# A chunked RWKV-7 recurrence: from two 64-column products per head pair to one 128x128 product each, with the outputs summed in SBUF

## The chip, the core and the metric

The kernel runs on one core of a Trainium2 chip. The metric is the device time of one execution in microseconds (us). The times given are the median of three runs with the lowest and the highest; the profile is of one further execution, and its own time stands beside its span.

The engines are called as the profile calls them: PE is TensorE (matmuls; PEld is its loading of weights), DVE is VectorE, ACT is ScalarE, POOL is GpSimd, SP is SyncE, whose queue issues nearly all DMAs.

## The reference

One layer of a hybrid decoder on 512 prompt tokens and 8 single decode tokens (520 columns in all), D_MODEL 2048. A shared RMS norm and one wide projection `w_in` feed two branches, an RWKV-7 time-mixing branch with 16 heads of 64 and a Conformer convolution branch; both are projected, merged by sigmoid gates, projected again, and a per-layer embedding and a last RMS norm follow. The part that the change touches is the state recurrence of the RWKV branch over the prompt:

```python
def _wkv7_scan(S0, r, w, k, v, a, b):
    def step(S, inp):
        r_t, w_t, k_t, v_t, a_t, b_t = inp
        sa = jnp.einsum('bhij,bhj->bhi', S, a_t)
        S = S * w_t[:, :, None, :] + sa[..., None] * b_t[:, :, None, :] + v_t[..., None] * k_t[:, :, None, :]
        return S, jnp.einsum('bhij,bhj->bhi', S, r_t)
...
S, o = _wkv7_scan(wkv_prev, rf, hd(decay), kf, vf, -kk, kk * hd(a))
mu = jnp.mean(o, axis=-1, keepdims=True)
var = jnp.mean(jnp.square(o - mu), axis=-1, keepdims=True)
o = ((o - mu) * lax.rsqrt(var + GN_EPS)).reshape(Bn, T, D_A) * lnx_g + lnx_b
```

The kernel does not step through the tokens. It cuts the 512 prompt tokens into 8 chunks of 64 and does each chunk with matrix products; `S` is carried from chunk to chunk.

## The kernel before

**The stream of big products.** All projections run through `step` (lines 195 to 213). A step takes one 128x128 block of weights, split into a high and a low part (`wh`, `wl`), and two halves of 260 columns of the activations, split likewise (`xh`, `xl`, or `hi`, `lo`), and issues six matmuls at line 211. `gemm` (line 215) makes 16 or 8 steps into one output tile. The weights come as 512 KB loads (line 143); ScalarE writes the high part (line 154), VectorE the low part (through the helper at line 107, which the profile shows as line 67, as all calls through `Paced`).

**The order of the work.** TensorE's order is the order of the program text (line 73), and from line 349 on VectorE's too. Everything that is not the stream is written as generators: `wkv(p, box)` for each of the 8 head pairs, `conv` for the convolution, and the tail (`samples`, `lnorm`, `reload`). After each step of `gemm`, `tick()` (line 181) lets each generator go on: `yield n` waits n steps, `yield ROOM` waits until the kernel's own estimate of VectorE's time is less than 1 us ahead of that of TensorE. These estimates grow with the calls: `pe_work` adds 0.13 us for each matmul of more than 32 columns, `vec` a price for each VectorE operation.

**The recurrence, `wkv` (line 427).** A head pair lies on the 128 partitions: head 0 on 0 to 63, head 1 on 64 to 127 (`half(h)`). For each pair:

- Lines 511 to 522 make `ar[h]` and `bk`. Lines 531 to 545 multiply them in both heads and mask the results into `nba`, `nbr` (on the diagonal blocks of a zeroed 128x128, two buffers, line 411) and into the other half of `ar[h]`.
- Lines 547 to 597 invert the triangular 32x32 blocks: `nba` goes through DRAM (`nd`) into `ni`; `ti` starts from a constant, copied by ScalarE from `cst` (line 567); 31 steps on VectorE; back through DRAM (`td`) into `dtt`, transposed into `dt`. Lines 602 to 610 complete `ttb`, the 128x128 inverse of both heads.
- Lines 613 to 621 make `suv`, which holds for each head and chunk the state on one half of the partitions and the values `v` on the other. Lines 624 to 630 transpose `bk` into `bkt`.
- Lines 632 to 662 are the **chunk loop**, 8 chunks each. The opening block makes two products of 64 columns for both heads: one into `x`, one into `oc`. ScalarE copies the first to `xs` (line 641). Four steps later (`ly`; five for the last pair) the middle block multiplies by `ttb`, and ScalarE puts the result into `suv` (line 645). Four steps on, the closing block makes again two 64-column products per head, one that updates the state (`bkt`) and one that is added to `oc` in PSUM (`nbr`). VectorE writes the next state into `suv` (line 655), ScalarE scales it into `sf` (line 659), and after four more steps the next chunk opens.
- Lines 666 to 698 normalise `oc` by head and write the result to DRAM (`oa_d`).

PSUM: `aux` tiles of 512 f32 per partition, four buffers (line 79), shared by all small products; `oc` held one of them for the whole loop. SBUF: `gt` gives tiles from a shared ring of 14 buffers (line 352), `kq.tile(name=...)` a buffer of that name.

Of the kernel before, what the change touches and what calls it, by code (L numbers as in the profile page):

```python
# [9 lines left out]
F32 = mybir.dt.float32  # L10
F32R = mybir.dt.float32r
AF = mybir.ActivationFunctionType
ALU = mybir.AluOpType
# [4 lines left out]
P = 128  # L18
T = 520
NPR = 512  # L20
# [3 lines left out]
NCH = 8  # L24
# [10 lines left out]
C_ID, C_GM, C_RM, C_TT, N_CST = 0, 128, 320, 576, 832  # L35
# [35 lines left out]
def body(nc, tc, a):  # L71
    with ExitStack() as es:
# [20 lines left out]
        dma = nc.sync.dma_start  # L93
        act = nc.scalar.activation
# [8 lines left out]
        vec = Paced(nc.vector, lambda name, n: work(0.0069 * n if name == "reciprocal" else (0.2 if name == "scalar_tensor_tensor" else 0.14) + 0.00107 * n))  # L103
        gps = Paced(nc.gpsimd, lambda name, n: work(0.0014 * n if n > 64 else 0.05))
        pe = Paced(nc.tensor, pe_work)

        def tt(eng, out, x, y, op):
            eng.tensor_tensor(out, x, y, op=op)
# [119 lines left out]
        def half(h):  # L228
            return slice(64 * h, 64 * h + 64)
# [22 lines left out]
        o = pa.tile([P, 512], F32, name="aux", tag="aux")  # L252
# [24 lines left out]
        cst = cp.tile([P, N_CST], F32, name="cst")  # L277
# [5 lines left out]
        ttinit = cst[:, C_TT:C_TT + 256]  # L283

        def constants():
            dma(out=sums, in_=a["cst"][:, N_CST:].rearrange("p (a b) -> p a b", a=3))
            dma(out=prm, in_=a["prm"])
            dma(out=muss, in_=a["ssT"])
            dma(out=cst, in_=a["cst"][:, :N_CST])
# [6 lines left out]
        def aux(name="aux"):  # L296
            return pa.tile([P, 512], F32, name=name, tag="aux")
# [40 lines left out]
        raw = kq.tile([P, NCH, P], F32, name="bkt").rearrange("p c x -> p (c x)")[:, :T]  # L338
# [16 lines left out]
        def gt(name):  # L355
            return gp.tile([P, T], F32, name=name, tag="g")
# [54 lines left out]
        nbrs = [kq.tile([P, NCH, P], F32, name=f"nbr{i}") for i in range(2)]  # L411
        for x in (ttb, *nbrs):
            gps.memset(x, 0.0)
# [13 lines left out]
        def wkv(p, box):  # L427
# [101 lines left out]
            nbr = nbrs[p % 2]  # L529
            f2 = lambda x: x.rearrange("p c a t -> p c (a t)")  # L530
            for c0 in (0, 4):
                os = [aux().rearrange("p (c x) -> p c x", x=P) for _ in range(2)]
                for c in range(4):
                    for h in range(2):
                        pe.matmul(os[h][:, c, :], lhsT=bk[half(h), c0 + c].rearrange("p a t -> p (a t)"),
                                         rhs=ar[h][half(h), c0 + c].rearrange("p a t -> p (a t)"), start=True, stop=True)
                yield 1
                for h in range(2):
                    s, u, o = half(h), half(1 - h), os[h]
                    mk = lambda s, i, n: gmask[s, i:i + n].unsqueeze(1).to_broadcast([64, 4, n])  # L540
                    tt(vec, nba[s, c0:c0 + 4], o[s, :, h * 64:h * 64 + 64], mk(s, 0, 64), ALU.mult)
                    i = 64 * (1 - h)
                    tt(vec, nbr[s, c0:c0 + 4, h * 64:h * 64 + 64], o[s, :, i:i + 64], mk(s, 64, 64), ALU.mult)
                    tt(vec, f2(ar[h][u, c0:c0 + 4]), o[u], mk(u, 64 * h, P), ALU.mult)
                    yield ROOM

# [11 lines left out]
            bh = bk.rearrange("p c a t -> p c (a t)")  # L558
# [3 lines left out]
            for g in range(4):  # L562
                dma(out=ni[g * 32:(g + 1) * 32], in_=nd.rearrange("h c e s t -> (h c e) s t"))
            yield 14
            vec.memset(ni.rearrange("p s t -> p (s t)")[:, 0::33], 1.0)
            ti = kq.tile([P, 8, 32], F32, name="ti")
            act(ti.rearrange("p i t -> p (i t)"), ttinit, AF.Copy)
# [10 lines left out]
            dtt = kq.tile([P, NCH, 32], F32, name="dtt")  # L578
# [4 lines left out]
            dt = kq.tile([P, NCH, 32], F32, name="dt")  # L583
# [40 lines left out]
            bkt = kq.tile([P, NCH, P], F32, name="bkt")  # L624
            for c0 in (0, 4):
                o = aux().rearrange("p (c x) -> p c x", x=P)
                for c in range(4):
                    pe.transpose(o[:, c, :], bh[:, c0 + c, :], ident)
                act(bkt[:, c0:c0 + 4, :], o, AF.Copy)
            yield 7  # L630

            oc = aux("oc").rearrange("p (c x) -> p c x", x=64)
            sf = kq.tile([P, 64], F32, name="sf")
            for c in range(NCH):
                x = aux().rearrange("p (c x) -> p c x", x=64)
                for h in range(2):
                    pe.matmul(x[half(h), 0, :], lhsT=ar[h][:, c, h, :], rhs=suv[:, h, c, :], start=True, stop=True)
                for h in range(2):
                    pe.matmul(oc[half(h), c, :], lhsT=ar[h][:, c, 1 - h, :], rhs=suv[:, h, c, :], start=True, stop=False)
                xs = kq.tile([P, 64], F32, name="xs", bufs=2)  # L640
                act(xs, x[:, 0, :], AF.Copy)
                yield ly
                pe.matmul(x[:, 2, :], lhsT=ttb[:, c, :], rhs=xs, start=True, stop=True)
                for h in range(2):
                    act(suv[half(h), h, c, :], x[half(h), 2, :], AF.Copy)
                yield ly
                for h in range(2):
                    pe.matmul(x[half(h), 3, :], lhsT=bkt[:, c, h * 64:h * 64 + 64], rhs=suv[:, h, c, :], start=True, stop=True)
                for h in range(2):
                    pe.matmul(oc[half(h), c, :], lhsT=nbr[:, c, h * 64:h * 64 + 64], rhs=suv[:, h, c, :], start=False, stop=True)  # L650

                for h in range(2) if c + 1 < NCH else ():
                    s = half(h)
                    if c:
                        vec.scalar_tensor_tensor(suv[s, h, c + 1, :], x[s, 3, :], epl[s, c:c + 1], sf[s], op0=ALU.mult, op1=ALU.add)
                    else:
                        vec.tensor_scalar(suv[s, h, 1, :], x[s, 3, :], epl[s, 0:1], None, op0=ALU.mult)
                for h in range(2) if c + 1 < NCH else ():
                    act(sf[half(h)], suv[half(h), h, c + 1, :], AF.Copy, scale=epl[half(h), c + 1:c + 2])  # L659
                if c + 1 == NCH:  # L660
                    vec.scalar_tensor_tensor(sf, x[:, 3, :], epl[:, c:c + 1], sf, op0=ALU.mult, op1=ALU.add)
                yield ly
            flag["done"] = p
# [3 lines left out]
            o1 = gt("o1")[:, :NPR].rearrange("p (c x) -> p c x", x=64)  # L667
# [5 lines left out]
            tt(vec, o1, oc, bc(m[:, 0]), ALU.subtract)  # L673
            sq = gt("sq")[:, :NPR].rearrange("p (c x) -> p c x", x=64)
            act(sq, o1, AF.Square)
# [7 lines left out]
            for h in range(2):  # L683
                for e in range(2):
                    tt(vec, on[half(e), :, h * 64:h * 64 + 64], o1[half(h), e::2, :],
                       m[half(h), 1, e::2].unsqueeze(2).to_broadcast([64, 4, 64]), ALU.mult)
                yield ROOM
# [474 lines left out]
```

## Time and profile before

| | |
|---|---|
| Median of three runs | 1788.19 us (1786.9 to 1790.8) |
| The profiled execution: its time, its span | 1786.46 us, 1784.6 us |
| Mean granted clock of TensorE | 0.995 |
| TensorE busy | 1765.0 us, 15576 matmul passes |
| VectorE, ScalarE, GpSimd busy | 1227.9, 805.4, 200.5 us |
| Chunk loops run | from 202.9 us (first pair) to about 1121 us (last pair) |

In the views of groups a row gives line, engine, operation, tiles (out<-in), shape and count; then busy us and the mean ns of one; then the idle time of the engine before them and what ended it. The mean length of a matmul holds its fill and its way through the array, and neighbours overlap; what a matmul costs the stream is read from the starts. In the timeline a row gives start and length in us, engine, line, operation, tiles, shape and count.

### The profile page before, as it was taken

How to read it: one execution, taken by the hardware profiler on the slowest of the kernel's cores; microseconds unless marked ns; L12 is line 12 of the kernel's file. 1: busy time of each engine (PE TensorE's matmuls, PEld its weight loads, DVE VectorE, ACT ScalarE, POOL GpSimd, SP SyncE). 2: the span in 40 equal slices, each digit the busy share in tenths (PEclk: the TensorE clock that was granted, in tenths of full speed). 3: DMA queues.
4: the chain of work that ended last, by engine and by line, in shares of the span. 5: the costliest groups of instructions: out<-in, count | busy, mean ns of one | idle time of the engine just before them, and what ended most of it. 6: DMA issues, size and time to landing. Idle time of an engine off the chain costs nothing.

```text
span 1784.6 us, 37783 instructions
## 1 busy us (share of the span) xinstructions
PE 1765.0 (99%) x15576; PEld 1728.7 (97%) x15576; DVE 1227.9 (69%) x2307; ACT 805.4 (45%) x1524; POOL 200.5 (11%) x237
## 2 busy tenths in 40 slices
PE   9999999999999999999999999999999999999996
PEld 9999999999999999999999999999999999999996
DVE  7568898899898797887987977465444333335457
ACT  6735447356364463463463433454333222243344
POOL 1100100001001001010010333001122000011111
PEclk9999999999999999999999999999999999999998
DMA  7253232432332434324324444477556332253233
GB/s 236 79 135 94 83 116 81 123 97 86 111 105 76 125 99 97 111 81 113 100 85 110 136 143 137 144 229 238 183 188 191 119 112 92 94 201 95 86 105 109
DMA packets 121037, 220.49 MB, mean 124 GB/s; under 512 B 47888, under 2 KB 56208, under 8 KB 120864
## 3 DMA queue, kind: packets, MB, share of 16 engines
q1 hardware_dynamic: 119264, 216.47, 39.4%
q8 instruction: 122, 2.00, 0.5%
q10 hardware_dynamic: 1600, 1.60, 0.3%
q14 instruction: 51, 0.42, 0.1%
HBM read 188.69 MB, written 29.34 MB: 122 GB/s over the span
## 4 chain that ended last, share of the span: by engine, by line
PE 96%; DVE 2%; DMA 1%; issue 0%; ACT 0%; POOL 0%; POOLq 0%; DVEq 0%; ACTq 0%
PE mm L211 88%; PE aux L67 6%; PE aux L211 1%; PE oc L67 1%; DVE c L67 1%; DVE wl L67 0%; DMA c_d<-c 0%; DVE h L67 0%; DMA w<-in_win 0%; POOL h L67 0%; DMA x<-in_xT 0%; DVE rf L67 0%; DVE bv L67 0%; POOLq L1158 0%; PE aux L1056 0%
## 5 line engine op out<-in xcount | busy, mean ns | idle before, releaser
L154 ACT ACTIVATE wh<-w 128x512 fp32r<-128x512 f32 (+1 forms) x541 | 339.2, 628 | 559.8 <-PE mm L211 493.4
L211 PE MATMUL mm<-xh,wh 128*128 128x260 f32 x2784 | 584.2, 291 | 0.1
L211 PE MATMUL mm<-xh,wl 128*128 128x260 f32 x2784 | 562.0, 283 | 1.1 <-DVE wl L67 0.9
L211 PE MATMUL mm<-xl,wh 128*128 128x260 f32 x2784 | 561.5, 283 | 0.0
L67 DVE TENSOR_TENSOR wl<-w,wh 128x512 fp32r<-128x512 f32 (+1 forms) x541 | 374.5, 694 | 172.3 <-ACT wh L154 170.1
L211 PEld LDWEIGHTS mm<-xh,wh 128*128 128x128 f32 x2784 | 428.5, 189 | 11.5 <-ACT wh L154 0.6
L211 PEld LDWEIGHTS mm<-xh,wl 128*128 128x128 f32 x2784 | 428.9, 189 | 1.5 <-DVE wl L67 1.5
L211 PEld LDWEIGHTS mm<-xl,wh 128*128 128x128 f32 x2784 | 429.5, 189 | 0.1
L211 PE MATMUL mm<-hi,wl 128*128 128x260 f32 x1600 | 332.8, 283 | 0.0
L211 PE MATMUL mm<-hi,wh 128*128 128x260 f32 x1600 | 332.5, 283 | 0.0
L211 PE MATMUL mm<-lo,wh 128*128 128x260 f32 x1600 | 331.8, 282 | 0.0
L211 PEld LDWEIGHTS mm<-hi,wh 128*128 128x128 f32 x1600 | 251.5, 189 | 0.0
L211 PEld LDWEIGHTS mm<-lo,wh 128*128 128x128 f32 x1600 | 251.1, 188 | 0.0
L211 PEld LDWEIGHTS mm<-hi,wl 128*128 128x128 f32 x1600 | 250.1, 188 | 0.0
L67 DVE SCALAR_TENSOR_TENSOR c<-u,prm,c 128x482 f32<-128x482 f32 (+14 forms) x240 | 186.9, 779 | 3.6
L67 DVE TENSOR_TENSOR p<-mm,rs 128x520 f32<-128x520 f32 x78 | 54.0, 693 | 53.7 <-PE mm L211 52.6
L67 DVE TENSOR_TENSOR tm<-ti,ni 128x16 f32<-128x16 f32 (+30 forms) x248 | 77.2, 311 | 5.7
L67 DVE TENSOR_REDUCE ti<-tm 128x8 f32<-128x16 f32 (+30 forms) x248 | 73.6, 297 | 8.5
L67 POOL TENSOR_TENSOR sq<-hi,lo 128x520 f32<-128x520 f32 (+1 forms) x20 | 26.8, 1344 | 353.7 <-DVE one L67 184.0
L67 DVE TENSOR_TENSOR s<-mm,s 128x520 f32<-128x520 f32 x32 | 22.4, 700 | 61.2 <-PE mm L211 61.2
L659 ACT ACTIVATE sf<-suv,epl 64x64 f32<-64x64 f32 x112 | 38.6, 345 | 56.7 <-DVE suv L67 55.2
L67 DVE SCALAR_TENSOR_TENSOR suv<-aux,epl,sf 64x64 f32<-64x64 f32 x96 | 27.1, 283 | 53.9 <-PE aux L67 51.8
(235 smaller groups left out, 1542.3 us busy)
## 6 DMA issues: line engine op xcount, KB each, us to landing
w<-in_win SPq DMA_DIRECT2D x170, 512.0 KB, 3.7
w<-in_wout SPq DMA_DIRECT2D x32, 512.0 KB, 3.7
w<-in_wpg SPq DMA_DIRECT2D x24, 512.0 KB, 3.6
s<-sga_d SPq DMA_DIRECT2D x32, 260.0 KB, 3.2
w<-in_wpa SPq DMA_DIRECT2D x16, 512.0 KB, 3.6
w<-in_wpb SPq DMA_DIRECT2D x16, 512.0 KB, 3.8
wx<-in_wpg SPq DMA_DIRECT2D x32, 256.0 KB, 4.5
x<-in_xT SPq DMA_DIRECT2D x16, 260.5 KB, 6.1
```

The lines of the kernel that those rows point to most:

```text
L67: return f(*args, **kw)
L154: behind.append(act(wh[:, k], w[:, k], AF.Copy))
L211: nc.tensor.matmul(o[h], lhsT=w[:, used[0] % 4, :], rhs=x[:, h * HF:(h + 1) * HF], start=(k == 0 and i == 0), stop=(k == nk - 1 and i == 2))
L659: act(sf[half(h)], suv[half(h), h, c + 1, :], AF.Copy, scale=epl[half(h), c + 1:c + 2])
```

## The change

Each block of the chunk loop becomes one full-width product per head. `ar[h]` of a chunk already holds both 64-column operands side by side, so the opening product takes all 128 columns: one half of its output partitions is what went into `x`, the other what went into `oc`. For the closing step a new operand `bn` (two buffers, zeroed once, 16 KB per partition together) holds for each chunk and head the 128 columns: the transposed `bk` and the masked product that was `nbr`. One `aux` tile `yy` serves two chunks. Its parts for `oc` no longer meet in PSUM: after every second chunk ScalarE copies the opening parts of two chunks into `oc`, now in SBUF and with the heads on swapped halves, and VectorE adds the closing parts. The last state update is done per head.

Besides: the transposes of `bk` move ahead of the inversion, as two groups of four with a pause of two steps behind each, and the pause of 7 steps before the loop goes; `ti` is loaded from DRAM by a DMA on SP's queue and not copied from `cst`, which shrinks by 256 columns; `dtt`, `dt` and `raw` share buffers with `ti`, `tm` and `ni`; the normalisation works in place on `oc`.

```diff
-        nbrs = [kq.tile([P, NCH, P], F32, name=f"nbr{i}") for i in range(2)]
-        for x in (ttb, *nbrs):
+
+        bns = [kq.tile([P, NCH, 2, 2, 64], F32, name=f"bn{i}") for i in range(2)]
+        for x in (ttb, *bns):
             gps.memset(x, 0.0)
...
-                    tt(vec, nbr[s, c0:c0 + 4, h * 64:h * 64 + 64], o[s, :, i:i + 64], mk(s, 64, 64), ALU.mult)
+                    tt(vec, bn[s, c0:c0 + 4, h, 1 - h, :], o[s, :, i:i + 64], mk(s, 64, 64), ALU.mult)
                     tt(vec, f2(ar[h][u, c0:c0 + 4]), o[u], mk(u, 64 * h, P), ALU.mult)
                     yield ROOM
+
+            for c0 in (0, 4):
+                o = aux().rearrange("p (c x) -> p c x", x=P)
+                for c in range(4):
+                    pe.transpose(o[:, c, :], f2(bk)[:, c0 + c, :], ident)
+                act(bn[:, c0:c0 + 4].rearrange("p c h a x -> p c (h a) x")[:, :, 0::3, :],
+                    o.rearrange("p c (h x) -> p c h x", h=2), AF.Copy)
+                yield 2
...
             for g in range(4):
                 dma(out=ni[g * 32:(g + 1) * 32], in_=nd.rearrange("h c e s t -> (h c e) s t"))
+            ti = kq.tile([P, 8, 32], F32, name="ti")
+            dma(out=ti, in_=a["cst"][:, C_TT:C_TT + 256].rearrange("p (i t) -> p i t", t=32))
             yield 14
             vec.memset(ni.rearrange("p s t -> p (s t)")[:, 0::33], 1.0)
-            ti = kq.tile([P, 8, 32], F32, name="ti")
-            act(ti.rearrange("p i t -> p (i t)"), ttinit, AF.Copy)
             yield 3
...
-            bkt = kq.tile([P, NCH, P], F32, name="bkt")
-            for c0 in (0, 4):
-                o = aux().rearrange("p (c x) -> p c x", x=P)
-                for c in range(4):
-                    pe.transpose(o[:, c, :], bh[:, c0 + c, :], ident)
-                act(bkt[:, c0:c0 + 4, :], o, AF.Copy)
-            yield 7
-
-            oc = aux("oc").rearrange("p (c x) -> p c x", x=64)
+            oc = gt("oc")[:, :NPR].rearrange("p (c x) -> p c x", x=64)
             sf = kq.tile([P, 64], F32, name="sf")
             for c in range(NCH):
-                x = aux().rearrange("p (c x) -> p c x", x=64)
+
+                if c % 2 == 0:
+                    yy = aux().rearrange("p (c i h x) -> p c i h x", c=2, i=2, h=2)
+                y, z = yy[:, c % 2, 0], yy[:, c % 2, 1]
+                xs = kq.tile([P, 64], F32, name="xs", bufs=2)
                 for h in range(2):
-                    pe.matmul(x[half(h), 0, :], lhsT=ar[h][:, c, h, :], rhs=suv[:, h, c, :], start=True, stop=True)
+                    pe.matmul(y[:, h, :], lhsT=ar[h][:, c].rearrange("p a t -> p (a t)"), rhs=suv[:, h, c, :], start=True, stop=True)
                 for h in range(2):
-                    pe.matmul(oc[half(h), c, :], lhsT=ar[h][:, c, 1 - h, :], rhs=suv[:, h, c, :], start=True, stop=False)
-                xs = kq.tile([P, 64], F32, name="xs", bufs=2)
-                act(xs, x[:, 0, :], AF.Copy)
+                    act(xs[half(h)], y[half(h), h, :], AF.Copy)
+                for h in range(2) if c % 2 else ():
+                    act(oc[half(1 - h), c - 1:c + 1], yy[half(1 - h), :, 0, h], AF.Copy)
                 yield ly
-                pe.matmul(x[:, 2, :], lhsT=ttb[:, c, :], rhs=xs, start=True, stop=True)
+                pe.matmul(z[:, 0, :], lhsT=ttb[:, c, :], rhs=xs, start=True, stop=True)
                 for h in range(2):
-                    act(suv[half(h), h, c, :], x[half(h), 2, :], AF.Copy)
+                    act(suv[half(h), h, c, :], z[half(h), 0, :], AF.Copy)
                 yield ly
                 for h in range(2):
-                    pe.matmul(x[half(h), 3, :], lhsT=bkt[:, c, h * 64:h * 64 + 64], rhs=suv[:, h, c, :], start=True, stop=True)
+                    pe.matmul(z[:, h, :], lhsT=bn[:, c, h].rearrange("p a x -> p (a x)"), rhs=suv[:, h, c, :], start=True, stop=True)
+
                 for h in range(2):
-                    pe.matmul(oc[half(h), c, :], lhsT=nbr[:, c, h * 64:h * 64 + 64], rhs=suv[:, h, c, :], start=False, stop=True)
-
-                for h in range(2) if c + 1 < NCH else ():
                     s = half(h)
-                    if c:
+                    if c + 1 == NCH:
+                        vec.scalar_tensor_tensor(sf[s], z[s, h, :], epl[s, c:c + 1], sf[s], op0=ALU.mult, op1=ALU.add)
+                    elif c:
...
                 yield ly
+                for h in range(2) if c % 2 else ():
+                    u = half(1 - h)
+                    tt(vec, oc[u, c - 1:c + 1], oc[u, c - 1:c + 1], yy[u, :, 1, h], ALU.add)
             flag["done"] = p
```

More of the change, by code (lines that the diff above doesn't have):

```diff
@@ L33 @@
 O_CW, O_CB, O_CG, O_CBB, O_FG, N_PRM = 81, 329, 337, 345, 353, 369
-C_ID, C_GM, C_RM, C_TT, N_CST = 0, 128, 320, 576, 832
+C_ID, C_GM, C_RM, N_CST, C_TT, C_SUM = 0, 128, 320, 576, 576, 832
 GROUPS = ([range(2 * _g, 2 * _g + 2) for _g in range(8)],
@@ L282, in body @@
         rmask = cst[:, C_RM:C_RM + 256]
-        ttinit = cst[:, C_TT:C_TT + 256]
         def constants():
-            dma(out=sums, in_=a["cst"][:, N_CST:].rearrange("p (a b) -> p a b", a=3))
+            dma(out=sums, in_=a["cst"][:, C_SUM:].rearrange("p (a b) -> p a b", a=3))
             dma(out=prm, in_=a["prm"])
@@ L337, in body @@
                 step(k, KD, xn[k], [first[m][h][:, :HF] if m > 1 else first[m][:, h, :HF] for h in range(2)], (0, 1))
-        raw = kq.tile([P, NCH, P], F32, name="bkt").rearrange("p c x -> p (c x)")[:, :T]
+        raw = kq.tile([P, 32, 32], F32, name="ni").rearrange("p s t -> p (s t)")[:, :T]
         act(v2(raw), first[0][:, :, :HF], AF.Copy)
@@ L528, in wkv @@
             nba = kq.tile([P, NCH, 64], F32, name="nba")
-            nbr = nbrs[p % 2]
+            bn = bns[p % 2]
             f2 = lambda x: x.rearrange("p c a t -> p c (a t)")
@@ L557, in wkv @@
             dma(out=sv_d.rearrange("v b c -> (v b) c")[:, p * P:(p + 1) * P], in_=st)
-            bh = bk.rearrange("p c a t -> p c (a t)")
             epl = kq.tile([P, NCH], F32, name="epl", bufs=2)
@@ L577, in wkv @@
                 dma(out=td.rearrange("h c e i t -> (h c e) i t")[:, g * 8:(g + 1) * 8, :], in_=ti[g * 32:(g + 1) * 32])
-            dtt = kq.tile([P, NCH, 32], F32, name="dtt")
+            dtt = kq.tile([P, NCH, 32], F32, name="ti")
             for h in range(2):
@@ L582, in wkv @@
             yield 18
-            dt = kq.tile([P, NCH, 32], F32, name="dt")
+            dt = kq.tile([P, NCH, 32], F32, name="tm")
             vec.transpose(dt, dtt)
@@ L649, in wkv @@
                 for h in range(2):
-                    pe.matmul(oc[half(h), c, :], lhsT=nbr[:, c, h * 64:h * 64 + 64], rhs=suv[:, h, c, :], start=False, stop=True)
-                for h in range(2) if c + 1 < NCH else ():
                     s = half(h)
-                    if c:
-                        vec.scalar_tensor_tensor(suv[s, h, c + 1, :], x[s, 3, :], epl[s, c:c + 1], sf[s], op0=ALU.mult, op1=ALU.add)
+                    if c + 1 == NCH:
+                        vec.scalar_tensor_tensor(sf[s], z[s, h, :], epl[s, c:c + 1], sf[s], op0=ALU.mult, op1=ALU.add)
+                    elif c:
+                        vec.scalar_tensor_tensor(suv[s, h, c + 1, :], z[s, h, :], epl[s, c:c + 1], sf[s], op0=ALU.mult, op1=ALU.add)
@@ L656, in wkv @@
                     else:
-                        vec.tensor_scalar(suv[s, h, 1, :], x[s, 3, :], epl[s, 0:1], None, op0=ALU.mult)
+                        vec.tensor_scalar(suv[s, h, 1, :], z[s, h, :], epl[s, 0:1], None, op0=ALU.mult)
                 for h in range(2) if c + 1 < NCH else ():
                     act(sf[half(h)], suv[half(h), h, c + 1, :], AF.Copy, scale=epl[half(h), c + 1:c + 2])
-                if c + 1 == NCH:
-                    vec.scalar_tensor_tensor(sf, x[:, 3, :], epl[:, c:c + 1], sf, op0=ALU.mult, op1=ALU.add)
@@ L666, in wkv @@
             bc = lambda x: x.unsqueeze(2).to_broadcast([P, NCH, 64])
-            o1 = gt("o1")[:, :NPR].rearrange("p (c x) -> p c x", x=64)
             m = kq.tile([P, 2, NCH], F32, name="m")
@@ L672, in wkv @@
             yield 2
-            tt(vec, o1, oc, bc(m[:, 0]), ALU.subtract)
+            tt(vec, oc, oc, bc(m[:, 0]), ALU.subtract)
             sq = gt("sq")[:, :NPR].rearrange("p (c x) -> p c x", x=64)
-            act(sq, o1, AF.Square)
+            act(sq, oc, AF.Square)
             yield 3
@@ L684, in wkv @@
                 for e in range(2):
-                    tt(vec, on[half(e), :, h * 64:h * 64 + 64], o1[half(h), e::2, :],
-                       m[half(h), 1, e::2].unsqueeze(2).to_broadcast([64, 4, 64]), ALU.mult)
+                    tt(vec, on[half(e), :, h * 64:h * 64 + 64], oc[half(1 - h), e::2, :],
+                       m[half(1 - h), 1, e::2].unsqueeze(2).to_broadcast([64, 4, 64]), ALU.mult)
                 yield ROOM
```

## Prediction

> **What bounds the kernel now.** I read the page first: the engines, the 40 slices, and the chain that ended last; then the waits of TensorE.
>
> ```profile
> span 1784.6 us, 37783 instructions
> PE 1765.0 (99%) x15576; PEld 1728.7 (97%) x15576; DVE 1227.9 (69%) x2307; ACT 805.4 (45%) x1524; POOL 200.5 (11%) x237
> PE   9999999999999999999999999999999999999996
> PEclk9999999999999999999999999999999999999998
> PE 96%; DVE 2%; DMA 1%; issue 0%; ACT 0%; POOL 0%; POOLq 0%; DVEq 0%; ACTq 0%
> ```
> ```profile
> 1196.90 551.80 PE mm L211 x4599
> ```
> ```profile
> PE aux L67 <- ACT suv L645: 2.2, 1, 2.2
> PE mm L211 <- DVE wl L67: 0.9, 1, 0.9
> PE aux L67 <- ACT xs L641: 0.2, 1, 0.2
> ```
>
> TensorE has work in every slice at the full granted clock, 96% of the chain is its own, and inside the recurrence it waited three times, 3.3 us together. So the time is the sum of what TensorE issues: a matmul taken out, or made cheaper, counts in full, and work on other engines counts only once TensorE waits for it. The middle row, from the chain in order of time, gives the pace of undisturbed products: 551.80 / 4599 = 0.120 us each. I measure every other block by how far it delays that pace. The busy column is no measure of it: matmuls overlap, so I go from start to start.
>
> **What the change takes out.** In each of 8 x 8 chunks of the recurrence TensorE has an opening block (state products for `xs` and `oc`), a middle one (`ttb`) and a closing one (`bkt`, `nbr`), with four steps of the big product (24 matmuls) behind each. First an opening block in the timeline of TensorE; the columns are start, length, engine, line, tiles, shape, count. An f32 matmul is recorded as two passes, so x4 is two matmuls.
>
> ```profile
> 202.62 0.40 PE L211 MATMUL mm<-xh,wl 128*128 128x260 f32 x2
> 202.95 0.34 PE L67 MATMUL aux<-suv,ar 128*64 128x64 f32 x4
> 203.11 0.29 PE L67 MATMUL oc<-suv,ar 128*64 128x64 f32 x4
> 203.33 0.51 PE L211 MATMUL mm<-xh,wh 128*128 128x260 f32 x2
> 203.67 0.40 PE L211 MATMUL mm<-xl,wh 128*128 128x260 f32 x2
> ```
> ```profile
> 206.08 0.40 PE L211 MATMUL mm<-xh,wl 128*128 128x260 f32 x2
> 206.31 0.33 PE L67 MATMUL aux<-xs,ttb 128*128 128x64 f32 x2
> 206.45 0.48 PE L211 MATMUL mm<-xh,wh 128*128 128x260 f32 x2
> 206.78 0.40 PE L211 MATMUL mm<-xl,wh 128*128 128x260 f32 x2
> ```
> ```profile
> 196.70 0.40 PE L211 MATMUL mm<-xh,wl 128*128 128x260 f32 x2
> 196.94 1.04 PE L67 MATMUL aux<-cst,bk 128*128 128x128 f32 x8
> 197.73 0.48 PE L211 MATMUL mm<-xh,wh 128*128 128x260 f32 x2
> 198.05 0.40 PE L211 MATMUL mm<-xl,wh 128*128 128x260 f32 x2
> ```
>
> Without the block the pair `xl,wh` would start two pairs, 0.48 us, after `xh,wl`. The opening block: 203.67 - 202.62 - 0.48 = 0.57 us for eight 64-column passes. The middle block: 206.78 - 206.08 - 0.48 = 0.22 us for two 128x128 passes, 0.110 each. Eight transposes, 128x128 weights too: 198.05 - 196.70 - 0.48 = 0.87, 0.109 each. Two passes and eight cost the same apiece, so a 128x128 pass has no fixed price to speak of.
>
> The 64-column block is different. Two of its four groups, as the view of groups by form has them (busy us, mean ns):
>
> ```profile
> L67 PE MATMUL aux<-suv,bkt 128*64 128x64 f32 x256 | 21.5, 246 | 2.2 <-ACT suv L645 2.2
> L67 PE MATMUL oc<-suv,ar 128*64 128x64 f32 x256 | 18.4, 222 | 0.0
> ```
>
> Its last pass is 0.222 long and ends at 203.11 + 0.29 = 203.40, so it started at 203.18: eight passes start within 0.23 us of the first, far below eight at 0.109. They run two at a time, one head on each column half. The remaining 0.34 us of the 0.57 lies at the edges: the block starts 0.33 after the pair before it (0.24 is normal), and the products behind it start late. The full-width blocks start on time.
>
> The closing block is read from a whole quiet chunk, from opening to opening:
>
> ```profile
> 532.96 0.34 PE L67 MATMUL aux<-suv,ar 128*64 128x64 f32 x4
> 542.98 0.34 PE L67 MATMUL aux<-suv,ar 128*64 128x64 f32 x4
> ```
>
> 10.02 us, less 72 x 0.120 = 8.64, leaves 1.38 for three blocks; less 0.22 for the middle leaves 1.16, or 0.58 for each of the other two.
>
> **What it puts in their place.** Each becomes two full-width matmuls, four passes with the shape of `ttb` (128x128 weights, 64 columns moving): 4 x 0.110 = 0.44. A chunk gains 1.16 - 0.88 = 0.28, and 64 chunks **17.9 us**. Bounds by the nearest rows: at the pace of a 260-column product, 0.120, a pass makes the gain 64 x (1.16 - 0.96) = 12.8; if a full pass cost no more than a pair of halves inside the old block, 0.23 / 4 = 0.06, 64 x (1.16 - 0.48) = 43. I take 0.110, because `ttb` is the same shape in the same place.
>
> **The rest, off TensorE's sum unless a wait comes of it.** The eight transposes a head pair stay eight; they move ahead into two groups of four: nothing. Durations for the other engines:
>
> ```profile
> 203.35 0.22 ACT L641 ACTIVATE xs<-aux 128x64 f32<-128x64 f32 x1 [2.01 <-PE aux L67]
> ```
> ```profile
> L641 ACT ACTIVATE xs<-aux x64: 202/224/227, 203.4 to 1113.5; 128x64 f32<-128x64 f32 x64
> ```
> ```profile
> L645 ACT ACTIVATE suv<-aux x128: 198/219/223, 206.7 to 1117.6; 64x64 f32<-64x64 f32 x128
> L619 ACT ACTIVATE suv<-aux x32: 377/379/384, 192.4 to 1017.0; 64x256 f32<-64x256 f32 x32
> ```
> ```profile
> L567 ACT ACTIVATE ti<-cst x8: 402/403/417, 32.6 to 877.8; 128x256 f32<-128x256 f32 x8
> L577 SPq DMA_DIRECT2D td<-ti x32: 317/413/1092, 168.9 to 991.4; - x32
> ```
> ```profile
> L67 DVE SCALAR_TENSOR_TENSOR suv<-aux,epl,sf 64x64 f32<-64x64 f32 x96 | 27.1, 283 | 53.9 <-PE aux L67 51.8
> L67 DVE TENSOR_TENSOR nbr<-aux,cst 64x256 f32<-64x256 f32 x32 | 13.3, 414 | 0.0
> ```
> ```profile
> 285.00:400.00 115.00, 115.00 (x1077) 110.81 (x1075) 99.64 (x212) 59.13 (x123) 9.28 (x18) 1.00 0.35 102
> ```
>
> *ScalarE.* `xs` becomes two copies of 0.22: 64 more, +14.1 us. Each odd chunk adds two 64x128 copies to `oc`, between 0.22 (64x64) and 0.38 (64x256), I take 0.27: 64 of them, 17.3 us. The `ti` copy goes, -3.2. Together +28 us over some 910 (first to last chunk in the `suv` row), on an engine busy 59 of 115 us (fourth pair in the window row). *VectorE.* Two 64x128 additions every odd chunk, between 0.28 and 0.41, I take 0.32: 64 of them, 20.5; the split last step adds 8 x 0.28. Together +23 us on an engine busy 99.6 of 115. Its conv work is handed out by the kernel's own clock, and four matmul charges fewer per chunk make that clock slower, so VectorE gets later conv work rather than a longer queue.
>
> *What hides it.* After the opening block ScalarE has until `ttb` at 206.31; `xs` started at 203.35 and took 0.22, so 2.7 us are free. I take it that `ttb`, which writes the PSUM tile that the new copies read, also waits for the `oc` copies: an odd chunk then uses 0.22 + 2 x 0.27 = 0.76 more, and 1.9 are left. Queued behind them on ScalarE are weight copies (`wh`) that run ahead. If the cover is gone, an odd chunk costs at most that 0.76: 32 x 0.76 = 24 us. Covered, nothing; I take nothing, since only one of 64 chunks waited for `xs`.
>
> *SP.* Eight loads of `ti`, 128 KB each, behind the `ni` loads and ahead of the next weights. One such issue holds the queue for 0.3 to 1.1 us by the `td` row, and `ti` is next used after 14 steps, ten microseconds later: hidden; uncovered 8 x 1.1 = 9 us. *POOL.* The buffers to be zeroed are twice as large:
>
> ```profile
> L67 POOL MEMSET nbr<- x2: 951/951/951, 1.6 to 2.5; 128x1024 f32 x2
> ```
> two more microseconds there, a hundred before their first use. *Memory.* `oc` leaves PSUM for a buffer of the shared ring where `o1` stood, held one loop longer. No row shows a wait for that ring; I take nothing, and up to rival 1's price if it comes.
>
> Sum, on the profiled execution: 1786.46 - 17.9 = 1768.6. That execution lies 1.7 under the median of the three runs, so against 1788.19 it is **1770.3 us**.
>
> **Rivals.**
> 1. *ScalarE's copies, or a shifted queue, make TensorE wait.* For it: the third wait row, and the 2.2 us one on `suv`, where ScalarE stood behind a late load; an odd chunk now has less slack in such places. Against: the 2.7 us above. A few such places give back 4 to 14 us: about 1779.
> 2. *Slower: the edges stay.* The two column halves ran side by side, 0.23 us in all; four passes in a row take 0.44. If the 0.34 us of edges belonged to the f32 blocks as such, a block would cost 0.44 + 0.34 = 0.78, and 128 x (0.78 - 0.575) = +26 us: about 1814. It decides where more than 0.135 of the 0.34 stays. Against: `ttb` and the transposes show almost none. The Trainium skill (TensorEngine Tiling (Array Packing), Overview and Tiling Modes) speaks for this side with "up to 2x" for narrow operands, and for mine with its rule that changing the tiling mode drains the engine; the starts within 0.23 us bear out the first, the edges the second.
> 3. *Nothing.* Both forms load 8 x 64 = 4 x 128 columns of weights. If columns alone set the cost, the new block costs what the old one does, 0.57, and the time stays 1788. Against: at 0.109 per 128 columns the old block would be 0.44, and it is 0.57. The Trainium skill (TensorE: Matmul & The Clock Gate, section LDWEIGHTS) states that rule, about columns / 1.2 in ns; by it alone this change is worth zero, and the 0.57 row says it isn't alone.
> 4. *More than I sum.* The four narrow groups hold 2 x (21.5 + 18.4) = 80 us of busy time, of which my blocks own 74; at the cheap bound (43) about 1745.
> 5. *The tail comes late.* The last branch's operands were ready at 1273.76 + 0.69, their first product ended at 1289.80:
>
> ```profile
> 1273.76 0.69 DVE L67 TENSOR_TENSOR lo<-c,hi 128x520 fp32r<-128x520 f32 x1
> 1289.80 0.70 DVE L67 TENSOR_TENSOR s<-mm,s 128x520 f32<-128x520 f32 x1 [1.75 <-PE mm L211]
> ```
>    15 us of room; conv work deferred by more would leave TensorE idle there, some 5 us: 1775.
>
> **How the numbers follow.** The largest wait of before, in the last pair's loop, cost more than itself:
>
> ```profile
> 1029.00:1034.00 5.00, 2.90 (x23) 2.49 (x21) 4.89 (x8) 1.43 (x4) 0.00 (x0) 1.00 0.50 161
> 1034.00:1040.00 6.00, 5.78 (x40) 5.58 (x42) 5.42 (x10) 2.12 (x5) 0.00 (x0) 0.72 0.69 190
> ```
>
> 5.00 - 2.90 = 2.1 us idle, then 6.00 us at a clock of 0.72, another 1.7: about 4 us. Forecast 0.75, its own range 1766 to 1775: one such place gone or come. Rival 1: 0.12; 2: 0.03; 3: 0.04; 4: 0.03; 5: 0.03. The range, 1763 to 1781, leaves out rivals 2 to 4 and the far end of 1. A measurement of this kernel tells 0.2% (3.6 us) from no change; faster by more are the forecast, 4, 5 and nearly all of 1: 0.91; within it 3 and a rest of 1: 0.05; slower 2 and a rest: 0.04.
>
> **What would show it.** The `suv,ar` groups would have shape 128*128 and start 0.24 after the pair before; `xl,wh` would come 0.92 us after `xh,wl` instead of 1.05; a quiet chunk would last 9.74 us. Waits of TensorE on `xs` in odd chunks would show rival 1, on `lo` of the last branch rival 5. I am wrong if a quiet chunk stays near 10.02, or if it shrinks and the span doesn't.

## The result, and the profile after

The changed kernel takes **1775.72 us** (median of 4 runs, 1775.46 to 1776.98), against 1787.67 (1786.9 to 1790.8, 4 runs) for the kernel before in the same comparison. The ratio is 0.9931, with a 95% interval of 0.9914 to 0.9948. That is 12.0 us of the 17.9 that were forecast. The profiled execution took 1775.46 us, 1773.7 of it span.

The page of the changed kernel: span, engines, the slices of TensorE and the chain that ended last.

```profile
span 1773.7 us, 36966 instructions
PE 1749.6 (99%) x15064; PEld 1738.9 (98%) x15064; DVE 1249.7 (70%) x2379; ACT 831.9 (47%) x1644; POOL 200.0 (11%) x237
PE   9999999999999999999999899999999999999996
PE 95%; DVE 3%; DMA 1%; issue 0%; ACT 0%; POOL 0%; SPq 0%; POOLq 0%; ACTq 0%; DVEq 0%
```

TensorE has 512 passes fewer, the eight per chunk that the change takes out. ScalarE has 26.5 us more work and VectorE 21.8 (the forecast had 28 and 23). One slice, the 23rd, is no longer full: 976 to 1020 us, where the last pair's chunk loop opens.

**The blocks came out as forecast.** First the timeline of TensorE at a closing block, then the opening products of a quiet chunk and of the next one, all of the changed kernel.

```profile
206.92 0.40 PE L211 MATMUL mm<-xh,wl 128*128 128x260 f32 x2
207.16 0.55 PE L67 MATMUL aux<-suv,bn 128*128 128x64 f32 x4
207.52 0.48 PE L211 MATMUL mm<-xh,wh 128*128 128x260 f32 x2
207.85 0.40 PE L211 MATMUL mm<-xl,wh 128*128 128x260 f32 x2
...
544.37 0.55 PE L67 MATMUL aux<-suv,ar 128*128 128x64 f32 x4
...
554.12 0.55 PE L67 MATMUL aux<-suv,ar 128*128 128x64 f32 x4
```

The block starts 0.24 us after the pair before it, and `xl,wh` comes 207.85 - 206.92 = 0.93 after `xh,wl`: the block costs 0.93 - 0.48 = 0.45. The quiet chunk lasts 9.75 us (forecast 9.74). From the starts of all such blocks the median is 0.446 after and 0.577 before, so 128 blocks are worth 16.8 us.

**What was given back** stands in TensorE's waits over the whole run (total, times, longest):

```profile
PE aux L67 <- ACT xs L642: 3.5, 1, 3.5
...
PE mm L211 <- DVE wl L67: 1.7, 2, 1.5
...
PE aux L67 <- ACT yt L601: 1.1, 2, 1.0
PE mm L211 <- DVE lo L67: 1.1, 1, 1.1
PE aux L67 <- DVE lo L67: 0.3, 1, 0.3
PE mm L211 <- ACT wh L154: 0.2, 1, 0.2
```

The two rows left out (2.1 on `sq`, 1.2 on `zero`) stand in both kernels. The rest is 7.9 us, against 2.2 + 0.9 + 0.2 = 3.3 before. And the waits cost more than themselves. The windows (PE, PEld, DVE, ACT and POOL busy, each with its count, then granted clock, DMA share, GB/s):

```profile
1001.00:1020.00 19.00, 12.86 (x126) 12.08 (x125) 18.65 (x22) 7.94 (x19) 9.15 (x6) 0.93 0.27 94
1017.30:1024.10 6.80, 4.85 (x22) 4.86 (x23) 6.69 (x11) 2.77 (x7) 0.00 (x0) 0.50 0.36 121
```

The granted clock was 0.50 for 6.80 us, from inside the longest wait on (that wait ends at 1019.25). TensorE was busy for 4.85 us of them, which costs half of that, 2.4; before, such a stretch cost 1.7. So waits and clock took 7.9 + 2.4 = 10.3 us after and 3.3 + 1.7 = 5.0 before: **5.3 us more**, and 16.8 - 5.3 = 11.5 is what the spans show within 0.6 us (1784.6 - 1773.7 = 10.9). The runs without conv 7, below, put it at 6.2. VectorE is busy 18.65 of the 19.00 us in the first window: there it is the bound.

The chain of waits in that stretch, in order of time (start, length, what), shows how the loss is made:

```profile
1007.19 1.77 DVE wl L67
1008.97 1.69 DVE c L67
...
1010.68 1.66 DVE c L67
...
1012.36 0.74 DVE c L67
...
1013.78 0.69 DVE wl L67
1014.47 0.66 DVE c L67
...
1017.36 0.70 DVE p L67
...
1018.08 0.05 ACT p L757
...
1018.74 0.22 ACT xs L642
...
1019.25 0.47 PE aux L67
```

and beside it GpSimd's timeline, the products of the sample branches:

```profile
1006.71 1.71 POOL L67 TENSOR_TENSOR s<-s,sv 128x512 f32<-128x512 f32 x1
1008.38 1.74 POOL L67 TENSOR_TENSOR t<-s,sv 128x512 f32<-128x512 f32 x1
1010.20 1.60 POOL L67 TENSOR_TENSOR s<-s,sv 128x512 f32<-128x512 f32 x1
```

While GpSimd multiplies, a conv step on VectorE (`c`, the eighth conv tile, called conv 7 below) takes 1.7 us; when it stops, at 1011.8, the same step takes 0.74. VectorE's queue is late by then: `wl` at 1013.78 stops TensorE for 1.5 us, and `p` comes at 1017.36. ScalarE's next instruction in program order is the scaling of `p`, and the copies to `xs`, whose product began at 1009.8, stand behind it. ScalarE's timeline; the bracket has the idle time before the instruction and what ended it:

```profile
1018.08 0.64 ACT L757 ACTIVATE p<-p 128x520 f32<-128x520 f32 x1 [8.42 <-DVE p L67]
1018.74 0.45 ACT L642 ACTIVATE xs<-aux 64x64 f32<-64x64 f32 x2
```

The kernel before had the same crowding, at 1006 to 1020 us, and lost less by it. Why, the opening products of the last pair and conv 7 show, in the views of the two tiles (count: least, median and longest in ns, first to last start); first the kernel before, then the changed one.

```profile
L67 PE MATMUL aux<-suv,ar x12: 222/246/270, 1023.6 to 1052.2; 128*64 128x64 f32 x12
...
L67 DVE SCALAR_TENSOR_TENSOR c<-u,prm,c x30: 711/742/1759, 989.6 to 1034.2; 128x482 f32<-128x482 f32 x1, 128x483 f32<-128x483 f32 x1, 128x484 f32<-128x484 f32 x1, 128x485 f32<-128x485 f32 x1
```
```profile
L67 PE MATMUL aux<-suv,ar x16: 217/275/275, 1009.8 to 1053.5; 128*128 128x64 f32 x16
...
L67 DVE SCALAR_TENSOR_TENSOR c<-u,prm,c x29: 683/739/1874, 989.0 to 1031.5; 128x483 f32<-128x483 f32 x1, 128x484 f32<-128x484 f32 x1, 128x485 f32<-128x485 f32 x1, 128x486 f32<-128x486 f32 x1
```

TensorE's gain over seven pairs brings the last pair's loop forward by 1023.6 - 1009.8 = 13.8 us, but VectorE's conv 7 ends only 2.7 earlier, and GpSimd's products some 9. Before, the loop opened when the products were over; now it opens among them.

The Trainium skill (SBUF — State Buffer, section "SBUF: two separate sides") says that a VectorE operation with two SBUF inputs and a GpSimd operation that reads SBUF lock a shared port pair against each other for a whole instruction. The steps of 1.7 us beside products of 1.7, and of 0.74 without, agree with it.

### The profile page after: what moved, and what is told of

Read it like the earlier page. It is cut to its first block, busy times and chain, and to the rows that moved or that the text cites. A ratio compares the mean times of both kernels' runs of the same rounds, so it can differ in the third digit from the quotient of the medians.

```text
span 1773.7 us, 36966 instructions
## 1 busy us (share of the span) xinstructions
PE 1749.6 (99%) x15064; PEld 1738.9 (98%) x15064; DVE 1249.7 (70%) x2379; ACT 831.9 (47%) x1644; POOL 200.0 (11%) x237
## 4 chain that ended last, share of the span: by engine, by line
PE 95%; DVE 3%; DMA 1%; issue 0%; ACT 0%; POOL 0%; SPq 0%; POOLq 0%; ACTq 0%; DVEq 0%
PE mm L211 87%; PE aux L67 7%; PE aux L211 1%; DVE c L67 1%; DVE wl L67 1%; DMA w<-in_win 1%; DVE h L67 0%; DVE tm L67 0%; DVE ti L67 0%; POOL h L67 0%; DMA s<-in_swkv 0%; DMA x<-in_xT 0%; ACT wh L154 0%; ACT sq L846 0%; DVE sq L67 0%
## 5 line engine op out<-in xcount | busy, mean ns | idle before, releaser
L67 POOL TENSOR_TENSOR sq<-hi,lo 128x520 f32<-128x520 f32 (+1 forms) x20 | 26.5, 1330 | 353.9 <-DVE one L67 184.0
```

The lines of the kernel that those rows point to most:

```text
L67: return f(*args, **kw)
```

## The experiments

Two readings were to be told apart: that the blocks gain what was forecast and the meeting of conv 7 with GpSimd and the loop gives a third of it back, or that the work added on ScalarE and VectorE does. Ratios are against the kernel before, each with its 95% interval.

### Conv 7 spread out, after and before

In the conv loop, of the changed kernel (e1) and of the kernel before (e2):

```diff
                 vec.scalar_tensor_tensor(c[:, d:NPR], u[:, 0:NPR - d], cw[:, k:k + 1], c[:, d:NPR], op0=ALU.mult, op1=ALU.add)
+                if i == 7:
+                    yield 3
                 yield ROOM
```

> The changed kernel, with the last convolution (conv 7) given out at most once in four steps. Theory A: the blocks gain the 16.7 us that the trace shows (128 x 0.13) and about 6 us are given back where conv 7 and the decode samples meet at the last pair: VectorE's queue fills, TensorE waits 6.7 us at 1001 to 1019 us and then runs 6.8 us at half clock. Without that meeting the time falls from 1775.7 to 1765-1769, and TensorE's waits there are under 1 us. Theory B: the give-back is the added copies and additions, spread over all loops: the time stays within 2 us of 1775.7.

> The kernel before, with the same spreading of conv 7. Theory A: it loses its own waits at 1020 to 1038 us (3.7 us idle, 1.7 us of half clock), so 1787.7 falls to 1781-1784, and the distance to the changed kernel with the same spreading is 15-18 us. Theory B: the distance stays about 12 us.

After: 1781.72 us, ratio 0.9974 (0.9963 to 0.9985), 6.0 slower than the change. Before: 1791.61, ratio 1.0024 (1.0015 to 1.0033). Both missed what was expected of them. The last pair's waits went, but conv 7 now ended at about 1080 us (1093 in e2) and the closing branches came late. The waits of TensorE in the changed kernel with conv 7 spread out, and the window of its tail:

```profile
PE mm L211 <- DVE lo L67: 5.2, 6, 2.4
PE mm L211 <- ACT hi L959: 4.4, 2, 3.2
```
```profile
1171.40:1191.80 20.40, 12.91 (x46) 10.64 (x47) 13.99 (x22) 9.52 (x16) 0.00 (x0) 0.50 0.53 174
```

20.4 us at half clock, TensorE busy for 12.9 of them: a larger loss at the end than the one that went. The distance of the two runs, 9.9 us, tells nothing of the blocks. With one step in place of three (e7, `yield 1`):

> The changed kernel, conv 7 given out at most once in two steps, where the spreading by four made the tail late. Theory A: the queue at the last pair is thinner and the tail not yet late: 1765-1772. Rival: no better than 1775.

1775.62 us, ratio 0.9933 (0.9918 to 0.9948): no change. ScalarE's wait for `p` fell from 8.4 us to 4.6 and TensorE's for `xs` from 3.5 to 1.6, but 3.4 us of waits on `lo` came at the tail, and there the granted clock was 0.50 from 1177.5 to 1187.7 us.

### Column halves again, in one block and in both

The copies to `oc` and the additions stay; only the products go back to 64 columns, in the closing block (e3), then in the opening block too (e4):

```diff
                 for h in range(2):
-                    pe.matmul(z[:, h, :], lhsT=bn[:, c, h].rearrange("p a x -> p (a x)"), rhs=suv[:, h, c, :], start=True, stop=True)
+                    for e in range(2):
+                        pe.matmul(z[half(e), h, :], lhsT=bn[:, c, h, e, :], rhs=suv[:, h, c, :], start=True, stop=True)
```
```diff
                 for h in range(2):
-                    pe.matmul(y[:, h, :], lhsT=ar[h][:, c].rearrange("p a t -> p (a t)"), rhs=suv[:, h, c, :], start=True, stop=True)
+                    for e in range(2):
+                        pe.matmul(y[half(e), h, :], lhsT=ar[h][:, c, e, :], rhs=suv[:, h, c, :], start=True, stop=True)
```

> The changed kernel, with each full-width closing product issued as two 64-column halves; all else is as changed. Theory A (width alone, 0.445 against 0.577 us a block): closing blocks cost 0.57 us again, 64 x 0.13 = 8.4 us, 1784 plus or minus 3 for the waits at the last pair. Rival (the edges belong to the f32 blocks or to their place, not to the column halves): the closing block stays near 0.45 and the time within 2 us of 1775.7.

> The changed kernel, with opening and closing products both as 64-column halves, so only the off-TensorE part of the change is left. Theory A: 128 x 0.13 = 16.7 us more than 1775.7, about 1792, that is 4-6 us above the kernel before: the price of what the change moves on the other engines. Rival (nothing is lost off TensorE): 1787-1788, as before.

Closing block alone: 1777.21 us, ratio 0.9943 (0.9928 to 0.9958). Both: 1782.82, ratio 0.9977 (0.9967 to 0.9987). The timeline of TensorE with both blocks split, one opening block:

```profile
554.94 0.40 PE L211 MATMUL mm<-xh,wl 128*128 128x260 f32 x2
555.27 0.45 PE L67 MATMUL aux<-suv,ar 128*64 128x64 f32 x8
555.65 0.51 PE L211 MATMUL mm<-xh,wh 128*128 128x260 f32 x2
555.99 0.28 PE L211 MATMUL mm<-xl,wh 128*128 128x260 f32 x1
```

The block starts 0.33 us after the pair before it, and costs 555.99 - 554.94 - 0.48 = 0.57 again: the edges belong to the column halves. By the starts of all blocks, e3 has 0.448 in the opening block and 0.577 in the closing one, e4 0.577 in both.

The blocks came as expected, the times did not: 1784 and 1792 us had been forecast. e3 gave up half of the blocks' gain, 8.4 us, and lost 1.5; e4 gave up all 16.8 and lost 7.1. Both got back what the change gives back. The waits of e4 beside `sq` and `zero`:

```profile
PE mm L211 <- ACT wh L154: 0.8, 1, 0.8
PE aux L67 <- DVE lo L67: 0.6, 1, 0.6
```

With two more of 0.2 that is 1.8 us in all, with no half clock ahead of the last 14 us (where every run has one), and with every added copy and addition in place: 10.3 - 1.8 = 8.5 us less than in the change, of the 9.7 between 16.8 and 7.1. So the added work as such isn't what costs. In these two runs the last pair's loop opened at 1023.9 and 1030.5 us, behind the products.

e4 also was 4.4 us faster than the kernel before (1787.18 in that comparison), though its blocks cost the same: it escaped the last-pair waits that the kernel before has. And splitting the products changes one thing beside the width: the kernel's planner counts 0.13 us for each matmul, so in e3 and e4 its clock of TensorE gets back the charges that the change had taken out.

### Without conv 7, after and before

```diff
-            for k in range(30):
+            for k in range(30 if i < 7 else 0):
```

> The changed kernel without the 30 taps of the last convolution tile on VectorE (that part of the output is left out). Theory A (the give-back is VectorE's queue at the last pair: conv 7 beside the decode samples): TensorE's waits at the last pair and behind the merges go, 9 to 11 us, so 1775.7 becomes 1765-1767. Rival (late weight loads or ScalarE's added copies make TensorE wait there): the waits stay, 1773-1777.

> The kernel before, the same 30 taps left out. Theory A: it loses its 5.4 us of waits and half clock at the last pair, 1787.4 becomes 1781-1783, and the distance to the changed kernel without the taps is the blocks' 16.7 us, within 1.5. Rival: the distance stays near 12.

The 30 steps of conv 7 are left out, and with them that part of the output. After: **1764.58 us**, ratio 0.9869 (0.9855 to 0.9884). Before: **1782.77**, ratio 0.9971 (0.9961 to 0.9982). The distance is 18.2 us (17.7 in the spans), near the 17.9 of the forecast, in a stream with next to no waits. The blocks are 16.8 of it, and waits that only the kernel before keeps 0.6 (1.1 against 0.5 beside `sq` and `zero`); the rest has no row here, so that the two numbers meet so closely is partly luck. Conv 7 costs the kernel before 1787.67 - 1782.77 = 4.9 us and the changed one 1775.72 - 1764.58 = 11.1. The difference, 6.2, is what was given back. Without it neither kernel has a wait of TensorE in the last pair's first 25 us, and the changed one none on `lo` at the tail.

The starts of all big matmuls, taken one by one in both runs of a kernel, show where conv 7 costs it. The kernel before loses about 5.3 us in the last pair's loop and next to nothing at the tail; the changed one loses 9.1 in the loop and 2.6 at the tail, between 1184 and 1190 us. So the loss has two places, and the tail has a larger share of it than the 1.6 us of waits there say.

### The copies to `oc` moved, the planner's price of a matmul raised

e9 puts the two `oc` copies behind the `sf` copies of the closing block. e8 leaves them and raises what a matmul outside the big product counts on the planner's clock of TensorE; e10 does both; e11 adds to e10 a later start of the samples.

```diff
-                for h in range(2) if c % 2 else ():
-                    act(oc[half(1 - h), c - 1:c + 1], yy[half(1 - h), :, 0, h], AF.Copy)
                 yield ly
...
                     act(sf[half(h)], suv[half(h), h, c + 1, :], AF.Copy, scale=epl[half(h), c + 1:c + 2])
+                for h in range(2) if c % 2 else ():
+                    act(oc[half(1 - h), c - 1:c + 1], yy[half(1 - h), :, 0, h], AF.Copy)
```
```diff
         def pe_work(name, n):
-            clock["pe"] += 0.13 if n > 32 else 0.04
+            clock["pe"] += 0.22 if n > 32 else 0.04
```
```diff
         def rest():
-            yield 12
+            yield 24
```

> The changed kernel, with the planner's price of a small matmul raised from 0.13 to 0.22 us, near what a two-pass 128x128 product takes. Theory: the change made the planner's clock of TensorE run slow by some 0.45 us a chunk against the trace, and with the right price VectorE's work comes earlier and off the tail: waits behind the merges go, 1770-1774. Rival: VectorE is overbooked more at the last pair: 1776-1782.

> The changed kernel with the copies of the opening parts to oc moved behind the closing block, where no product waits for the tile they read. The block costs stay. Theory A (the give-back is VectorE's queue at the last pair): little to gain in the quiet loops, 1773-1778. Rival (the added copies on ScalarE are what gives back): 1766-1770.

> The changed kernel with both: oc copies behind the closing block and 0.22 us as the planner's price of a small matmul. In the run with the price alone TensorE waited 1.1 us for an oc copy at 544 us; that wait goes: 1769-1771 against 1771.4. Rival: the order on ScalarE shifts and another wait takes its place, 1772 or more.

> As the run before, and the decode samples start 12 steps later in the last pair's loop, so that more of conv 7 is done when GpSimd begins. Theory A: fewer waits at the last pair, 1766-1769; the tail keeps its room. Rival: the tail gets late, 1772 or more.

| | median, us | ratio (95%) |
|---|---|---|
| e8, price 0.22 | 1771.43 | 0.9907 (0.9891 to 0.9924) |
| e9, copies later | 1776.49 | 0.9939 (0.9924 to 0.9953) |
| e10, both | **1769.92** | 0.9903 (0.9888 to 0.9917) |
| e11, and samples 12 steps later | 1770.96 | 0.9912 (0.9895 to 0.9928) |

e9 has the waits of the change unaltered (3.5 on `xs`, 1.5 on `wl`, 6.8 us at half clock): the copies to `oc` give nothing back there. With the higher price the planner's clock runs faster, and conv 7's last step starts at 1026.3 us (e8) and 1024.9 (e10) instead of 1031.5. In both the first chunk's `xs` copies come ahead of `p` in ScalarE's queue, and neither run has a stretch at half clock ahead of the last 14 us. Both loops open earlier than that of the change, at 1007.2 us (e8) and 1006.1 (e10), and in e10 GpSimd's products go on until 1013.5. The opening products of e10, then its waits in the whole run:

```profile
L67 PE MATMUL aux<-suv,ar x20: 217/275/323, 1006.1 to 1057.0; 128*128 128x64 f32 x20
```

```profile
PE aux L67 <- DVE suv L67: 1.9, 1, 1.9
...
PE aux L67 <- ACT yt L601: 0.8, 2, 0.6
PE aux L67 <- ACT xs L642: 0.7, 1, 0.7
```

e10 is the fastest of the complete kernels: its slowest run (1770.13) lies 5.3 us below the fastest of the change (1775.46), and it is 17.1 us faster than the kernel before (1787.02 in that comparison). A chunk makes 9 small products in the kernel before and 5 in the changed one, so the change took the planner's charge for a chunk from 1.17 us to 0.65; at 0.22 it is 1.10 again. (The price counts for all small products, not only for those of the chunks.) So the planner's slower clock is a possible cause of the loss, and no run here separates it from the early opening. Starting the samples later (e11) adds nothing, where 1766 to 1769 us had been expected. e8 also answers a question of the forecast, whether the middle product waits for the `oc` copies. Its timelines, ScalarE and then TensorE (the brackets: idle before, and what ended it):

```profile
544.93 0.55 ACT L644 ACTIVATE oc<-aux 64x128 f32<-64x128 f32 x2
...
545.53 0.43 PE L67 MATMUL aux<-xs,ttb 128*128 128x64 f32 x2 [1.14 <-ACT oc L644]
```

It does, once in 32 odd chunks; the `xs` of that chunk had been there since 541.95. With the copies moved (e10) that wait is gone.

### Without GpSimd's products

The four GpSimd products of a sample step are left out, and with them the samples' outputs; VectorE's part reads `s0` in their place, and `work(0.0014 * 512)` keeps what the planner counts. An excerpt:

```diff
-                tt(gps, t1, s0, bc8(1), ALU.mult)
+                work(0.0014 * 512)
...
-                vec.tensor_reduce(sa, t1, axis=AX.X, op=ALU.add)
-                tt(gps, s0, s0, bc8(0), ALU.mult)
+                vec.tensor_reduce(sa, s0, axis=AX.X, op=ALU.add)
+                work(0.0014 * 512)
```

> The changed kernel without the decode samples' products on GpSimd (left out, their outputs with them); VectorE keeps its own part of the samples and all of conv 7, and the planner's prices stay. Theory A2 (VectorE's steps take up to 1.7 us instead of 0.75 beside GpSimd's, and that is what fills its queue): conv steps near 0.75 us at the last pair, TensorE's waits there fall from 6.7 us to under 2, 1765-1770. Rival (the planner hands VectorE too much even without GpSimd): conv steps at 0.75, but waits of 4 us or more stay, 1773 or more.

**1767.93 us**, ratio 0.9897 (0.988 to 0.9913): 7.8 faster than the change. The view of conv 7's tile, and the windows around the last pair's first chunks, in this run:

```profile
L67 DVE SCALAR_TENSOR_TENSOR c<-u,prm,c x30: 685/734/749, 984.9 to 1023.6; 128x482 f32<-128x482 f32 x1, 128x483 f32<-128x483 f32 x1, 128x484 f32<-128x484 f32 x1, 128x485 f32<-128x485 f32 x1
```
```profile
1001.00:1020.00 19.00, 18.77 (x183) 18.41 (x181) 18.44 (x29) 10.08 (x25) 0.00 (x0) 1.00 0.40 132
```

No conv step is longer than 0.749 us; TensorE is busy 18.77 us where it was busy 12.86, at full clock. VectorE is as busy as before (18.44): it gets more done. So 7.8 of the 11.1 us that conv 7 costs the changed kernel go back to GpSimd's products beside it (and to VectorE's waits for their results, which went with them). By the starts all of that is won in the last pair's loop; the tail's waits on `lo`, 1.1 and 0.3 us, stay, and so does what they cost. This run was not made for the kernel before, which has the same crowding, so it does not say how much of the 6.2 us is GpSimd's.

### How much lateness the loop bears

Put side by side, the runs whose loop opens at 1009 to 1011 us with a scaling of `p` ahead of `xs` give a price. In the changed kernel 30 big matmuls lie between the opening block and the middle one; at 0.120 each, with 0.45 for the block, TensorE reaches the middle product some 4.1 us after the opening started (an estimate; waits on `wl` come on top).

| | opening, us | wait of ScalarE for `p` | `xs` ready after opening | TensorE waits for `xs` |
|---|---|---|---|---|
| e12 | 1009.6 | 2.5 | 3.5 | 0 |
| e7 | 1010.4 | 4.6 | 5.6 | 1.4 |
| e9 | 1010.0 | 8.4 | 9.4 | 3.5 (and 1.5 for `wl`) |
| change | 1009.8 | 8.4 | 9.4 | 3.5 (and 1.5 for `wl`) |

5.6 - 4.1 = 1.5, and 9.4 - 4.1 - 1.5 = 3.8: within 0.3 us what TensorE waited, and the 3.5 of e12 is covered.

## Why the forecast was right, and where it was wrong

It was 1770.3 us, with a range of 1763 to 1781. The time lies in the range and 0.7 us above the forecast's own one.

- **What bounds the kernel**: right. The time went where TensorE's stream, its waits and its clock went, within 0.6 us.
- **What the change takes out, and what it puts in**: right. 0.577 and 0.446 us for a block (forecast 0.57 and 0.58, 0.44), a quiet chunk of 9.75. With the disturbance taken out of both kernels they lie 17.7 to 18.2 us apart.
- **Rivals 2 and 3** (the edges stay; columns alone set the cost): both false. e4 has every part of the change but the width (and the planner's count of matmuls), and its blocks cost 0.57. That agrees with the rule of the Trainium skill (TensorEngine Tiling (Array Packing), section Tiling Modes) that changing the mode drains the engine: 0.57 with the change of mode, 0.45 without.
- **Durations of the added work**: right. An `oc` copy 0.271 us (forecast 0.27), an addition 0.286 (0.32). The view of the tile `oc` in the changed kernel:

```profile
L644 ACT ACTIVATE oc<-aux x64: 259/271/273, 211.9 to 1102.1; 64x128 f32<-64x128 f32 x64
L67 DVE TENSOR_TENSOR oc<-oc,aux x64: 278/286/294, 223.7 to 1113.0; 64x128 f32<-64x128 f32 x64
```

- **"Covered, nothing"** was the term that failed, in the part on the rest, off TensorE's sum. Not by the added copies to `oc`: the longest wait on them in these runs is e8's 1.14 us, and the change itself has none. It took the 2.7 us of the first pair's first chunk for the slack of every chunk. In the last pair ScalarE's queue holds `p` ahead of `xs`, and `p` comes from a VectorE that GpSimd slows. The mechanism, TensorE as the sum of what it issues, held; the term, put at 0, measured 5.3 us by waits and clock and 6.2 by the runs without conv 7.
- **Rival 1** named the place (a shifted queue makes TensorE wait on `xs`) and a price, 4 to 14 us, that holds the 5.3 to 6.2; it was given 0.12. Its first half, ScalarE's copies, is not borne out: in e9 the `oc` copies move and the waits stay, in e4 all copies stay and the waits go. The 2.2 us wait that it argued from lies in the same loop, and the forecast read it as a fixed loss that comes or goes whole, "about 4 us". It turned from 4.8 us (2.2, 0.9 and 1.7 of slow clock) into 7.6 (0.2, 3.5, 1.5 and 2.4). That this came of the loop's move is argued, not shown.
- **Rival 5** (the tail): in part. Waits on `lo` and `wl` came to 1.6 us at the tail, and by the starts it lost about 2.6. The 15 us of room were read at the wrong place: that row is the last branch (`lo<-c`, at 1273.76), and the time was lost at the branch before it (`lo` of `y`, at 1184). Losses of the forecast's 5 us and more came only in e1, e2 and e7, where conv 7 was put off.
- **VectorE gets "later conv work rather than a longer queue"**: the first half was right and was the danger. Conv 7 moved forward by 2.7 us where the loop moved by 13.8, and with the higher price of e8 and e10 it moved by 5.2 and 6.6 more.

What is shown: that a block costs 0.13 us less by its width alone (e3, e4), that conv 7 costs the changed kernel 6.2 us more than the kernel before (e5, e6), that 7.8 of its 11.1 us go with GpSimd's products (e12), and that the `oc` copies are not the cause (e4, e9). What is argued: that the opening's move by 13.8 us is why the same crowding costs more. The openings of e3 and e4 and the table of lateness fit it, but no run moved the opening alone, and e8 and e10 open earlier still and lose less: there `xs` stands ahead of `p`. So the order in ScalarE's queue counts, and the early opening by itself is not enough. The planner's slower clock stays as a rival: its price was not tried in the kernel before, so what e10 gains by it cannot be split between this change and the kernel as it was.

## What to carry to other kernels

Where one engine bounds the stream, price an edit there by starts, and trust it; then look at where each slower-moving neighbour stands after the gain has added up. Here a gain of 0.26 us a chunk moved the last loop by 14 us, while VectorE's conv 7 moved by 2.7, and a third of the gain was lost in that loop and at the tail behind it. Ask for each in-order queue what stands ahead of the short copy that the bound engine waits for, and whether an order planned by estimates still has the estimates right.

## What was not expected of the hardware

- A conv step of VectorE (two SBUF inputs) took 1.6 to 1.9 us beside GpSimd's products and 0.749 at most without any (e12): more than twice as long, a full product's length at a time.
- The granted clock was 0.50 for 3.4 us in e3, from 2.3 us after the start of the products that a wait of 1.34 us had held up; in the change it was 0.50 for 6.8, from inside the 3.5 us wait on; after a single wait of 1.9 us in e10 it did not fall. The length of one wait does not decide it. In e3 32x32 products stood between the wait and the slow stretch. TensorE's timeline of e3, then windows:

```profile
302.45 0.24 PE L67 MATMUL aux<-tm,yt 32*32 32x32 f32 x2 [1.34 <-ACT yt L601]
302.85 0.69 PE L67 MATMUL aux<-tm,yt 32*32 32x32 f32 x30 [0.16 <-ACT yt L601]
```
```profile
298.00:304.80 6.80, 5.30 (x70) 4.94 (x69) 4.51 (x7) 6.64 (x13) 1.82 (x2) 1.00 0.13 27
304.80:308.20 3.40, 3.40 (x18) 3.40 (x17) 3.37 (x6) 2.57 (x7) 0.00 (x0) 0.50 0.68 223
```

- Four narrow groups that overlap two by two cost 0.57 us, 0.34 of it at the edges; the same products as one wide group 0.45. The mean lengths said the opposite (222 to 246 ns narrow, 261 wide): only the starts of the neighbours showed it.
